# Order of the split products and a finer issue of transposes in a two-layer decoder trunk

## The chip, the cores and the metric

One core of one Trainium2 chip runs the whole program in a single launch. The metric is the device time of one execution in microseconds; the median of three runs of the kernel before is 2433.37 us (2432.49 to 2433.54).

## The reference

Two decoder layers over 256 tokens of width 2048, in float32. Layer 0 mixes with gated linear attention beside RWKV-7, layer 1 with causal softmax attention of 16 heads and an ALiBi penalty; behind each mixer stands a SwiGLU FFN with 5632 hidden columns. Cut to what matters here:

```python
h = x
for layer in range(2):
    hn = rmsnorm(h, norm_mix[layer])
    h = h + (gla_rwkv_mixer(hn, ...) if layer == 0 else moba_attention(hn, attn_qkv_w[0], attn_out_w[0]))
    h = h + swiglu(rmsnorm(h, norm_ffn[layer]), ffn_gate_w[layer], ffn_up_w[layer], ffn_down_w[layer])
return rmsnorm(h, norm_final)

def swiglu(h, w_gate, w_up, w_down):
    return (silu(h @ w_gate) * (h @ w_up)) @ w_down
```

## The kernel before, in words

**Split products.** Each weight block arrives in float32 (`raw`, L135 to L141) and is split in two: ScalarE copies it to the rounded type, `hi` (L150), and VectorE subtracts to get `lo` (L151). The activations lie split too, transposed (128 features on the partitions, 256 tokens in columns), as `xh` and `xl`. A product is the sum of three matmuls: `xh` with `hi`, `xh` with `lo`, `xl` with `hi`. In mode "x" (L170 to L172) the activation is the stationary operand (128 x 128) and the weights move (512 columns), for two token halves `t` in two PSUM tiles; in mode "w" (L177 to L180: the mixer's first projections, queries and keys) the weights are stationary and 256 tokens move.

**Jobs and units.** `run_jobs` works through a list of jobs, one for each 512 output columns of a matrix. A job has units of two 128-row weight blocks: 24 matmuls in mode "w" and 12 in mode "x". A gate or up job has 8 units, a down job of an FFN group 12 (group one: hidden tiles 0 to 5, 24 blocks) or 10 (group two: tiles 6 to 10, 20 blocks). The split of a unit is issued AHEAD = 2 units before its products; `raw` has NRAW = 4 buffers, `hi` and `lo` three each. So the split of unit n+2 reuses the buffer that unit n-1 has read. The loads go out on the SP queue.

**Side work.** Everything else (evacuating PSUM, activations, norms, transposes, attention) is written as generators. Before each unit `tick()` takes one hop of every hot generator, and hops of the others while a budget of 1.80 lasts; a `yield` says what a hop is charged. All engines run in program order, so what a hop issues stands on VectorE and ScalarE ahead of the split issued behind it. `force` ticks on until a condition holds: at a job's first unit until the job two back has been evacuated, and in a down job (`ready`) until the hidden tile whose rows the unit reads has been split.

**The FFN.** For a hidden tile j comes a gate job, whose evacuation is a Silu on ScalarE (L1009), and an up job, whose evacuation multiplies (L1014), turns the tile into `hT` with VectorE's 32 x 32 block transposes (`quads`, L257, four instructions a call, eight calls a tile) and splits `hT` into `hth` (L1027) and `htl` (L1028). This generator runs in the units of the next job. Two calls of `quads` make one hop.

**The residual and the norms.** `t_add` adds a down job's output to `h` (L954), in the last group sums the squares, and makes the next block of `xh`, `xl`. For the second mixer's norm (`gmix1`, end of layer 0) blocks 0 to 2 are turned by `quads`, block 3 by TensorE (`xt_bank`: four transposes in a PSUM bank, L242); for the FFN norms all four blocks are turned by TensorE.

Of the kernel before, what the change touches and what calls it, by code (L numbers as in the profile page):

```python
# [10 lines left out]
F32 = mybir.dt.float32  # L11
# [7 lines left out]
P = 128  # L19
S = 256  # L20
# [26 lines left out]
def tile_trunk(  # L47
# [4 lines left out]
    V, A, T, G = nc.vector, nc.scalar, nc.tensor, nc.gpsimd  # L52
# [34 lines left out]
        return dict(w=w_ap, segs=segs or [(0, c0, 512)], ncol=ncol, rows=rows, x=x, done=done, mode=mode, start=start,  # L87
                    ready=ready)

    # Side work runs as generators: each yields what its hop is charged against a step's BUDGET.  # L90
    tasks = []
    carry = [0.0]
    flags = set()
# [31 lines left out]
    def run_jobs(jobs, prologue):  # L125
        BOTH = slice(0, 2)
        units = [(jb, i) for jb in jobs for i in range(0, len(jb["rows"]), 2)]
        raws, splits = {}, {}

        def fetch(n):  # L130
            if n >= len(units):
                return
            jb, i = units[n]
            raw = wpool.tile([P, 2, 512], F32, tag="raw", name="raw", bufs=NRAW)
            r0 = jb["rows"][i][1] * P  # L135
            for dst, c0, w in jb["segs"]:
                nc.sync.dma_start(
                    raw[:, :, dst : dst + w],
                    jb["w"][r0 : r0 + 2 * P, c0 : c0 + w].rearrange("(k p) n -> p k n", p=P),
                )  # L140
            raws[n] = raw  # L141

        def split(n, ks):
            if n >= len(units):
                return
            ncol = units[n][0]["ncol"]
            if n not in splits:
                splits[n] = tuple(wpool.tile([P, 2, 512], F32R, tag=g, name=g, bufs=3) for g in ("hi", "lo"))
            (hi, lo), raw = splits[n], raws[n]
            A.activation(hi[:, ks, :ncol], raw[:, ks, :ncol], AF.Copy)  # L150
            V.tensor_sub(lo[:, ks, :ncol], raw[:, ks, :ncol], hi[:, ks, :ncol].bitcast(F32))  # L151

        def finish(jb, k):
            yield from jb["done"](jb["pt"])
            flags.add(("evac", k))

        def products(n, k, ts=(0, 1)):
            jb, i = units[n]
            hi, lo = splits[n]
            xh, xl = jb["x"]()  # L160
            nm = jb["ncol"] // P
            if i + k == 0 and 0 in ts:
                jb["pt"] = [mm_tile() for _ in range(2)]
            pt = jb["pt"]
            xi = jb["rows"][i + k][0]
            first, last = i + k == 0, i + k == len(jb["rows"]) - 1
            if jb["mode"] == "x":
                for t in ts:
                    sl = slice(t * P, t * P + P)
                    T.matmul(pt[t], xh[:, xi, sl], hi[:, k, :], start=first, stop=False)  # L170
                    T.matmul(pt[t], xh[:, xi, sl], lo[:, k, :], start=False, stop=False)  # L171
                    T.matmul(pt[t], xl[:, xi, sl], hi[:, k, :], start=False, stop=last)  # L172
            else:
                for m in range(nm):
                    o = pt[m // 2][:, (m % 2) * 256 : (m % 2) * 256 + 256]
                    ms = slice(m * P, m * P + P)
                    T.matmul(o, hi[:, k, ms], xh[:, xi, :], start=first and m % 2 == 0, stop=False,  # L177
                             skip_group_check=True)
                    T.matmul(o, hi[:, k, ms], xl[:, xi, :], start=False, stop=False, skip_group_check=True)  # L179
                    T.matmul(o, lo[:, k, ms], xh[:, xi, :], start=False, stop=last, skip_group_check=True)  # L180

        for n in range(NRAW):
            fetch(n)
        prologue()
        for n in range(AHEAD):
            split(n, BOTH)
            fetch(n + NRAW)
            if n == 0:
                spawn(t_x0(), hot=True)
                tick()  # L190
        for half in range(2):
            spawn(t_chain_when(half))
            spawn(t_rwkv_e(half), fast=lambda half=half: (("kp", half) in flags and ("dec", half) in flags
                                                          and ("pre", half) not in flags)
                  or (("neu", half) in flags and ("inv", half) not in flags))
            spawn(t_rwkv_r(half))
            spawn(t_rwkv_d(half))
        spawn(t_gate())
        spawn(t_gla())
        for n, (jb, i) in enumerate(units):  # L200
            if i == 0 and jb["start"]:
                jb["start"]()
            tick()
            if i == 0:
                k = jobs.index(jb)
                if k >= 2:
                    force(lambda: ("evac", k - 2) in flags)
            busy = any(t[2] and t[2]() for t in tasks)
            if jb["ready"]:
                force(lambda: jb["ready"](jb["rows"][i + 1][0]))  # L210
            split(n + AHEAD, slice(0, 1) if busy else BOTH)
            if not busy:
                fetch(n + AHEAD + NRAW)
            if n == len(units) - 3:
                while tasks:
                    tick()
                for t in range(2):
                    for m in range(n, n + 3):
                        for k in range(2):
                            products(m, k, (t,))  # L220
                    jb["done"](t, jb["pt"][t])
                break
            products(n, 0)
            if busy:
                mid()
                split(n + AHEAD, slice(1, 2))
                fetch(n + AHEAD + NRAW)
            products(n, 1)
            if i + 2 >= len(jb["rows"]):
                spawn(finish(jb, jobs.index(jb)), hot=True)  # L230
        while tasks:
            tick()
# [33 lines left out]
        V.tensor_scalar(dst, dst, 1.0 / D, RMS_EPS, op0=ALU.mult, op1=ALU.add)  # L266
        half_pow(dst, dst)

    # ------------------------------------------------------------ layer 0 mixer: state
    right = ExitStack()  # L270
    st = {"right": right}
    opool = right.enter_context(tc.tile_pool(name="opool", bufs=1, side="right"))
# [103 lines left out]
    def quarter(pt, p):  # L376
        return pt[p // 2][:, (p % 2) * 256 : (p % 2) * 256 + 256]

    # ------------------------------------------------------------ layer 0 mixer: tasks
    def t_lora(pt):  # L380
        wa = wt([P, S], "t1")
        g1 = wt([P, S], "t2")
# [540 lines left out]
            yield 1.8  # L923
        flags.add(("og", j))

    # ------------------------------------------------------------ residual stream
    def open_h():
        left.close()
        hpool = ctx.enter_context(tc.tile_pool(name="hpool", bufs=1, reuse_waits="tile"))
# [19 lines left out]
    def t_add(j, gname=None, last=False, final=False):  # L949
        def go(pt):  # L950
            h = st["h"]
            for t in range(2):
                hs = h[:, t, j * 512 : j * 512 + 512]
                V.tensor_add(hs, pt[t], hs)  # L954
            if gname is not None or final:
                sumsq(h, j, st["junk"])
            yield 1.3
            if final:
                cols = slice(j * 512, j * 512 + 512)
                for t in range(2):  # L960
                    V.tensor_mul(st["ob"][:, t, cols], h[:, t, cols], st["nf"][:, cols])
                yield 1.2
            if last:
                rstd_of(rst)
            if gname == "gmix1" and not last:
                hT = st["fp"].tile([P, 4, S], F32, tag="hT", name="hT", bufs=2)
                for t in range(2):
                    for i in range(4):
                        quads(hT[:, :, t * P + 32 * i : t * P + 32 * i + 32],
                              h[32 * i : 32 * i + 32, t, j * 512 : j * 512 + 512].rearrange("p (f c) -> p f c", f=4))  # L970
                        if i % 2:
                            yield 1.6
                for b in range(2):
                    xt_evac(st["xh"], st["xl"], hT[:, 2 * b : 2 * b + 2, :].rearrange("p a t -> p (a t)"),
                            4 * j + 2 * b, gname)
                    yield 1.0
            elif gname is not None:
                for b in range(2):
                    xt_bank(st["xh"], st["xl"], h, 4 * j + 2 * b, gname)
                    yield 1.0  # L980
            if last and gname == "gmix1":
                flags.add("rst1")
        return go

    def final_rows(t, ps):
        h, ob, rt = st["h"], st["ob"], rst[:, t : t + 1]
# [15 lines left out]
    def t_gate_up(layer, kind, j, g0):  # L1002
        def go(pt):
# [15 lines left out]
            for t in range(2):  # L1019
                for i in range(4):  # L1020
                    quads(hT[:, :, t * P + 32 * i : t * P + 32 * i + 32],
                          sgt[32 * i : 32 * i + 32, t, :].rearrange("p (f h) -> p f h", f=4))
                    if i % 2:
                        yield 1.6
            for b in range(2):
                f, hb = (j - g0) * 4 + 2 * b, hT[:, 2 * b : 2 * b + 2, :]
                A.activation(hth[:, f : f + 2, :], hb, AF.Copy)  # L1027
# [40 lines left out]
                                 t_add(j, gnext if g0 else None, last=bool(g0) and j == 3, final=final)))  # L1068
        return jobs

    # ------------------------------------------------------------ layer 1 attention
    def open_attn():
        st["fs"].close()
        rs = ExitStack()
# [87 lines left out]
        flags.add(("head", hd))  # L1162
        yield 0.8

    # ------------------------------------------------------------ program
    with tc.manual_schedule():
        jobs = [gemm(mix_in, 0, ALLK, xT, t_lora, mode="w", segs=[(0, 6160, 256), (256, 6384, 64), (320, 3072, 64)])]
        for half in range(2):
# [120 lines left out]
```

## Time and profile before

| what | value |
|---|---|
| median of three runs | 2433.37 us |
| profiled execution, first to last instruction | 2431.0 us |
| TensorE busy, matmuls | 2383.2 us, 98% |
| VectorE busy | 1601.4 us, 66% |
| ScalarE busy | 1071.2 us, 44% |
| bytes read from HBM | 421.34 MB, 174 GB/s with those written |

The span is that of one profiled execution; the runs' times were taken by themselves. The profile counts an engine as busy from an instruction's start to its end; the ends of matmuls are modelled and lie behind the start of the next, so an idle time of TensorE reads shorter than the delay of the start. A number in brackets behind a timeline row is the engine's idle time before it and what ended it. x8 behind a row means eight like instructions in a run.

### The profile page before, as it was taken

The numbers are of one execution on the slowest core, as the hardware profiler recorded it, in microseconds if no ns is written. First come the engines' busy times: TensorE is split into PE (matmuls) and PEld (weight loads), VectorE is DVE, ScalarE is ACT, GpSimd is POOL, SyncE is SP. The second block draws the span as 40 slices with busy tenths as digits, with TensorE's granted clock in tenths as the row PEclk, the third lists the DMA queues.
The fourth block names the chain that finished last, engine by engine and source line by source line (L and its number), as shares of the span: only waits on it lengthen the run. The fifth ranks groups of instructions, "written<-read, shape, count | busy, mean of one in ns | idle before, by whom it ended". The sixth has DMA issues, their size and how long they took to land.

```text
span 2431.0 us, 33126 instructions
## 1 busy us (share of the span) xinstructions
PE 2383.2 (98%) x12786; PEld 2017.5 (83%) x12786; DVE 1601.4 (66%) x2505; ACT 1071.2 (44%) x1380; POOL 158.4 (7%) x183
## 2 busy tenths in 40 slices
PE   8999999999999999999999999999999999999998
PEld 8999978788787888887879999978887878887876
DVE  4765864666667644677785677886667664477664
ACT  5553454454444433444444444445444433444443
POOL 2270440100000000000000000000000000000000
PEclk9999999999999999999999999999999999999999
DMA  6542543555665655665556565555665655656654
GB/s 195 151 140 84 149 145 91 169 173 182 197 189 177 199 186 187 190 189 185 180 176 191 166 182 174 167 180 182 191 190 175 198 189 184 191 185 191 193 182 156
DMA packets 224094, 425.61 MB, mean 175 GB/s; under 512 B 17600, under 2 KB 19936, under 8 KB 223808
## 3 DMA queue, kind: packets, MB, share of 16 engines
q1 hardware_dynamic: 222976, 419.66, 55.2%
q0 software_dynamic: 960, 3.83, 0.5%
q8 instruction: 100, 1.64, 0.3%
q14 instruction: 58, 0.48, 0.1%
HBM read 421.34 MB, written 2.10 MB: 174 GB/s over the span
## 4 chain that ended last, share of the span: by engine, by line
PE 74%; DVE 20%; issue 3%; ACT 2%; DMA 0%; SPq 0%; ACTq 0%; POOLq 0%; POOL 0%; DVEq 0%
PE mmt L171 19%; PE mmt L172 19%; PE mmt L170 18%; DVE hT L257 9%; DVE lo L151 8%; PE mmt L177 4%; PE mmt L180 4%; PE mmt L179 4%; DVE pT L257 2%; ACT hi L150 2%; PE auxt L600 1%; DMA raw<-in_mix_in 0%; PE auxt L639 0%; PE auxt L632 0%; PE auxt L242 0%
## 5 line engine op out<-in xcount | busy, mean ns | idle before, releaser
L151 DVE TENSOR_TENSOR lo<-raw,hi 128x1024 fp32r<-128x1024 f32 (+2 forms) x818 | 973.6, 1193 | 738.4 <-ACT hi L150 732.1
L150 ACT ACTIVATE hi<-raw 128x1024 fp32r<-128x1024 f32 (+2 forms) x818 | 837.6, 1029 | 924.3 <-PE mmt L172 801.9
L171 PE MATMUL mmt<-lo,xh 128*128 128x512 f32 x1664 | 651.2, 391 | 16.5 <-DVE lo L151 16.5
L170 PE MATMUL mmt<-hi,xh 128*128 128x512 f32 x1664 | 652.3, 392 | 0.0
L172 PE MATMUL mmt<-hi,xl 128*128 128x512 f32 x1664 | 648.8, 390 | 0.0
L171 PEld LDWEIGHTS mmt<-lo,xh 128*128 128x128 f32 x1664 | 312.8, 188 | 91.1 <-DVE lo L151 28.1
L170 PEld LDWEIGHTS mmt<-hi,xh 128*128 128x128 f32 x1664 | 312.7, 188 | 65.6
L172 PEld LDWEIGHTS mmt<-hi,xl 128*128 128x128 f32 x1664 | 312.8, 188 | 64.1
L177 PE MATMUL mmt<-xh,hi 128*128 128x256 f32 x1072 | 312.9, 292 | 2.4 <-DVE xl L252 2.2
L180 PE MATMUL mmt<-xh,lo 128*128 128x256 f32 x1072 | 304.4, 284 | 4.1 <-DVE lo L151 4.1
L179 PE MATMUL mmt<-xl,hi 128*128 128x256 f32 x1072 | 303.6, 283 | 0.0
L171 PE MATMUL mmt<-lo,hth 128*128 128x512 f32 x704 | 280.3, 398 | 5.2 <-DVE lo L151 5.2
L170 PE MATMUL mmt<-hi,hth 128*128 128x512 f32 x704 | 279.1, 396 | 0.0
L172 PE MATMUL mmt<-hi,htl 128*128 128x512 f32 x704 | 279.0, 396 | 0.0
L257 DVE STREAM_TRANSPOSE hT<-sgt 32x128 f32<-32x128 f32 x704 | 212.8, 302 | 9.8
L180 PEld LDWEIGHTS mmt<-xh,lo 128*128 128x128 f32 x1072 | 205.7, 192 | 5.6 <-DVE lo L151 5.6
L177 PEld LDWEIGHTS mmt<-xh,hi 128*128 128x128 f32 x1072 | 205.8, 192 | 5.0 <-ACT hi L150 2.0
L179 PEld LDWEIGHTS mmt<-xl,hi 128*128 128x128 f32 x1072 | 205.9, 192 | 0.8
L171 PEld LDWEIGHTS mmt<-lo,hth 128*128 128x128 f32 x704 | 132.6, 188 | 41.9 <-DVE lo L151 10.2
L170 PEld LDWEIGHTS mmt<-hi,hth 128*128 128x128 f32 x704 | 132.6, 188 | 32.3
L172 PEld LDWEIGHTS mmt<-hi,htl 128*128 128x128 f32 x704 | 132.6, 188 | 31.8
L257 DVE STREAM_TRANSPOSE pT<-lg 32x96 f32<-32x96 f32 x256 | 69.0, 269 | 3.8
(291 smaller groups left out, 1667.8 us busy)
## 6 DMA issues: line engine op xcount, KB each, us to landing
raw<-in_wg SPq DMA_DIRECT2D x176, 512.0 KB, 3.5
raw<-in_wu SPq DMA_DIRECT2D x176, 512.0 KB, 3.6
raw<-in_wd SPq DMA_DIRECT2D x176, 512.0 KB, 3.6
raw<-in_mix_in SPq DMA_DIRECT2D x96, 512.0 KB, 3.6
raw<-in_qkv SPq DMA_DIRECT2D x96, 512.0 KB, 4.0
raw<-in_mix_out SPq DMA_DIRECT2D x32, 512.0 KB, 3.6
raw<-in_attn_out SPq DMA_DIRECT2D x32, 512.0 KB, 3.7
arz<-in_x SPq DMA_DIRECT2D x8, 256.0 KB, 5.8
```

The lines of the kernel that those rows point to most:

```text
L150: A.activation(hi[:, ks, :ncol], raw[:, ks, :ncol], AF.Copy)
L151: V.tensor_sub(lo[:, ks, :ncol], raw[:, ks, :ncol], hi[:, ks, :ncol].bitcast(F32))
L170: T.matmul(pt[t], xh[:, xi, sl], hi[:, k, :], start=first, stop=False)
L171: T.matmul(pt[t], xh[:, xi, sl], lo[:, k, :], start=False, stop=False)
L172: T.matmul(pt[t], xl[:, xi, sl], hi[:, k, :], start=False, stop=last)
L177: T.matmul(o, hi[:, k, ms], xh[:, xi, :], start=first and m % 2 == 0, stop=False, skip_group_check=True)
L179: T.matmul(o, hi[:, k, ms], xl[:, xi, :], start=False, stop=False, skip_group_check=True)
L180: T.matmul(o, lo[:, k, ms], xh[:, xi, :], start=False, stop=last, skip_group_check=True)
L257: V.transpose(dst[32 * q : 32 * q + 32], src[:, :, 32 * q : 32 * q + 32])
L600: T.matmul(psA[p // 2][:, (p % 2) * 256 : (p % 2) * 256 + 256], bk[:, p, c, :], arz[:, p, c, :, :], start=True, stop=True)
```

## The change

In mode "x" each weight block's four products with `hi` come first (both token halves), then the two with `lo`. The hop of the FFN tile's transposes has one call of `quads` and is charged 1.3. Of the blocks of the second mixer norm, block 0 is turned by `quads` in a hot generator of its own that does nothing in every other tick; blocks 1 and 2 go through `xt_bank`, as block 3 did. Some comment lines are taken out.

```diff
@@ products
                 for t in ts:
                     sl = slice(t * P, t * P + P)
                     T.matmul(pt[t], xh[:, xi, sl], hi[:, k, :], start=first, stop=False)
-                    T.matmul(pt[t], xh[:, xi, sl], lo[:, k, :], start=False, stop=False)
-                    T.matmul(pt[t], xl[:, xi, sl], hi[:, k, :], start=False, stop=last)
+                    T.matmul(pt[t], xl[:, xi, sl], hi[:, k, :], start=False, stop=False)
+                for t in ts:
+                    sl = slice(t * P, t * P + P)
+                    T.matmul(pt[t], xh[:, xi, sl], lo[:, k, :], start=False, stop=last)
@@ t_add
-            if gname == "gmix1" and not last:
-                hT = st["fp"].tile([P, 4, S], F32, tag="hT", name="hT", bufs=2)
-                for t in range(2):
-                    for i in range(4):
-                        quads(hT[:, :, t * P + 32 * i : t * P + 32 * i + 32],
-                              h[32 * i : 32 * i + 32, t, j * 512 : j * 512 + 512].rearrange("p (f c) -> p f c", f=4))
-                        if i % 2:
-                            yield 1.6
-                for b in range(2):
-                    xt_evac(st["xh"], st["xl"], hT[:, 2 * b : 2 * b + 2, :].rearrange("p a t -> p (a t)"),
-                            4 * j + 2 * b, gname)
-                    yield 1.0
+            if gname == "gmix1" and j == 0:
+                spawn(t_quads(gname), hot=True)
             elif gname is not None:
                 for b in range(2):
                     xt_bank(st["xh"], st["xl"], h, 4 * j + 2 * b, gname)
@@ new
+    def t_quads(gname):
+        h = st["h"]
+        hT = st["fp"].tile([P, 4, S], F32, tag="hT", name="hT", bufs=2)
+        for t in range(2):
+            for i in range(4):
+                yield 0
+                quads(hT[:, :, t * P + 32 * i : t * P + 32 * i + 32],
+                      h[32 * i : 32 * i + 32, t, 0:512].rearrange("p (f c) -> p f c", f=4))
+                yield 1.3
+        for b in range(2):
+            xt_evac(st["xh"], st["xl"], hT[:, 2 * b : 2 * b + 2, :].rearrange("p a t -> p (a t)"), 2 * b, gname)
+            yield 1.0
@@ t_gate_up
                 for i in range(4):
                     quads(hT[:, :, t * P + 32 * i : t * P + 32 * i + 32],
                           sgt[32 * i : 32 * i + 32, t, :].rearrange("p (f h) -> p f h", f=4))
-                    if i % 2:
-                        yield 1.6
+                    yield 1.3
```

## Rows read from the trace of the kernel before

**Rows 1.** The page's engine table: busy us, share of the span, instructions.
```profile
PE 2383.2 (98%) x12786; PEld 2017.5 (83%) x12786; DVE 1601.4 (66%) x2505; ACT 1071.2 (44%) x1380; POOL 158.4 (7%) x183
```

**Rows 2.** The page's costliest groups: count, busy, mean ns, idle before, releaser.
```profile
L171 PE MATMUL mmt<-lo,xh 128*128 128x512 f32 x1664 | 651.2, 391 | 16.5 <-DVE lo L151 16.5
```

**Rows 3.** TensorE's waits, whole span: us in total, times, longest us.
```profile
PE mmt L171 <- DVE lo L151: 23.3, 30, 2.2
```

**Rows 4.** TensorE's waits, four stretches in order: 552:816, 816:952, 952:1174, 1174:1293.
```profile
PE mmt L171 <- DVE lo L151: 4.0, 5, 0.8
...
PE mmt L171 <- DVE lo L151: 0.3, 1, 0.3
...
PE mmt L171 <- DVE lo L151: 3.2, 4, 0.8
...
PE mmt L171 <- DVE lo L151: 4.3, 7, 0.7
```

**Rows 5.** TensorE's timeline, gate and up tiles: start us, us, instruction, count [idle].
```profile
699.96 0.50 PE L171 MATMUL mmt<-lo,xh 128*128 128x512 f32 x1 [0.80 <-DVE lo L151]
...
742.34 0.39 PE L171 MATMUL mmt<-lo,xh 128*128 128x512 f32 x1
742.57 0.39 PE L172 MATMUL mmt<-hi,xl 128*128 128x512 f32 x1
...
743.47 0.39 PE L170 MATMUL mmt<-hi,xh 128*128 128x512 f32 x1
744.66 0.50 PE L171 MATMUL mmt<-lo,xh 128*128 128x512 f32 x1 [0.80 <-DVE lo L151]
```

**Rows 6.** VectorE's timeline, 733 to 749 us, the same tile.
```profile
739.57 1.23 DVE L151 TENSOR_TENSOR lo<-raw,hi 128x1024 fp32r<-128x1024 f32 x1
740.82 2.52 DVE L257 STREAM_TRANSPOSE hT<-sgt 32x128 f32<-32x128 f32 x8
743.38 1.23 DVE L151 TENSOR_TENSOR lo<-raw,hi 128x1024 fp32r<-128x1024 f32 x1
744.52 1.29 DVE L1028 TENSOR_TENSOR htl<-hT,hth 128x512 fp32r<-128x512 f32 x2
```

**Rows 7.** ScalarE's timeline, 738 to 758 us, the same tile.
```profile
743.38 1.15 ACT L1027 ACTIVATE hth<-hT 128x512 fp32r<-128x512 f32 x2 [4.13 <-DVE hT L257]
...
747.52 1.06 ACT L150 ACTIVATE hi<-raw 128x1024 fp32r<-128x1024 f32 x1 [1.09 <-PE mmt L172]
749.57 1.37 ACT L1009 ACTIVATE sgt<-mmt,rst 128x512 f32<-128x512 f32 x2 [0.98 <-PE mmt L172]
```

**Rows 8.** TensorE's timeline, two successive down jobs that end layer 0.
```profile
1217.98 0.50 PE L171 MATMUL mmt<-lo,hth 128*128 128x512 f32 x1 [0.60 <-DVE lo L151]
...
1248.02 0.50 PE L171 MATMUL mmt<-lo,hth 128*128 128x512 f32 x1 [0.60 <-DVE lo L151]
```

**Rows 9.** TensorE's timeline around one bank of transposes, 1661 to 1663 us.
```profile
1661.11 0.39 PE L172 MATMUL mmt<-hi,aol 128*128 128x512 f32 x1
...
1661.81 0.40 PE L172 MATMUL mmt<-hi,aol 128*128 128x512 f32 x1
1662.05 0.60 PE L242 MATMUL auxt<-cs__68,h 128*128 128x128 f32 x4
...
1662.71 0.40 PE L171 MATMUL mmt<-lo,aoh 128*128 128x512 f32 x1
```

**Rows 10.** Windows: us, busy of PE, PEld, DVE, ACT, POOL, PEclk, DMA, GB/s.
```profile
323.40:326.80 3.40, 3.40 (x10) 2.62 (x9) 2.14 (x2) 2.78 (x4) 3.12 (x4) 0.50 0.62 172
...
500.00:556.00 56.00, 56.00 (x260) 45.50 (x259) 36.21 (x48) 30.74 (x53) 0.70 (x1) 1.00 0.53 173
```

**Rows 11.** TensorE's timeline, 320 to 327 us, a value job of layer 0.
```profile
323.00 0.50 PE L171 MATMUL mmt<-lo,xh 128*128 128x512 f32 x1 [2.25 <-DVE lo L151]
...
324.10 0.63 PE L171 MATMUL mmt<-lo,xh 128*128 128x512 f32 x1
324.53 0.63 PE L172 MATMUL mmt<-hi,xl 128*128 128x512 f32 x1
```

**Rows 12.** TensorE's timeline, 1618 to 1622 us, attention's output projection.
```profile
1620.44 0.50 PE L171 MATMUL mmt<-lo,aoh 128*128 128x512 f32 x1 [1.58 <-DVE lo L151]
```

## The prediction

> **What bounds the kernel now.** I read the page's engine table first: TensorE is busy for 2383.2 of 2431.0 us [rows 1]. That number does not say how much can be won, because matmul records overlap: one 512-column matmul is recorded with 391 ns [rows 2], but in a quiet stretch the fifth after one at 742.34 starts at 743.47 [rows 5], 0.227 us each. So I go by start-to-start times. The kernel ends when TensorE has issued its matmuls, and only what lengthens that pitch costs time.
>
> Next, TensorE's waits. The one large entry is L171 (the low half of the split weights) waiting for VectorE's `lo`: 23.3 us in 30 waits [rows 3]. Asked by stretch, they sit in the first FFN and its end: five in gate/up tiles 0 to 5, one in the first down job, four in the second group's gate/up, seven in its down jobs [rows 4]. Layer 1 repeats the first three stretches with the same counts and times (its last down jobs, without the mixer norm, have only one wait).
>
> The timelines show why. In every gate/up tile VectorE runs eight 32x32-block transposes (2.50 us), then the next unit's `lo` (1.23 us): start to start 3.8 us, four units in a row [rows 6], while TensorE takes twelve matmuls, 12 x 0.227 = 2.72 us. VectorE falls behind by about 1.1 us a unit; with two units split ahead, the fourth is too late. L171 then starts 1.19 us after L170 instead of 0.227 [rows 5].
>
> **The change part by part.** The sum is against the profiled execution: its span is 2431.0 us; the median of the runs is 2433.37 us. I carry the 2.4 us between them unchanged.
>
> *Transposes four at a time (FFN tiles).* VectorE's unit becomes 4 x 0.313 + 1.23 = 2.5 us, under 2.72: it no longer falls behind. Price of one stall: two consecutive stalled matmuls stand at 699.96 and 744.66, 44.70 us apart [rows 5]; a tile has 16 units, 192 x 0.2267 = 43.52 us. So 1.18 us a tile, including the slow matmuls just behind the stall. 5 + 4 tiles per layer, 18 in all: -21.2 us. The wait in the first down job of each of four groups is shorter (0.3 us idle [rows 4] against 0.80; I price it 0.64, an estimate that takes off the 0.5 less of idling, its unit being 12 x 0.234 = 2.81 us): -2.6 us.
>
> What takes the place? Eight hops plus the first (the multiply), the split into high and low, and a last one that sets the flag make 11 ticks; a gate job has 8 units. So at unit 0 of the next up job the eighth hop is issued, and the demand that the job two back be evacuated forces the split into the same unit. There ScalarE has the Silu pair 1.37 us, the `hth` pair 1.15 and a `hi` of 1.06 [rows 7], then comes `lo` with 1.23: 4.8 us from the unit's start. That `lo` is first used two units and, in the new order, four matmuls later: 2 x 2.72 + 0.91 = 6.35 us. It is covered by 1.5 us; I cost it at nothing, and if the cover went, at up to the old 1.18 us a tile.
>
> In a group's first down job there is a real new wait. Group one has 24 rows; its last tile's rows are read at unit 10 and the split comes at unit 9: nothing. Group two has 20 rows; its last tile is read at unit 8, whose own tick issues the eighth hop, and the forced tick puts the split behind it. Worked out: `hi` of the unit ahead starts when its buffer is freed; 1.06 of `hi`, 1.23 of `lo` and 1.25 of four transposes are 3.54 us against a unit of 2.81; the transposes end 0.3 (buffer freed two matmuls earlier by the new order) to 0.7 us into unit 8. Then one `hth` (half of the 1.15 pair, 0.62 with its start) and one `htl` (half of the pair's 1.29 [rows 6], 0.69 with its start): TensorE's second matmul waits 1.5 to 2.0 us, with the slow restart about 1.9. Two layers: +3.8 us. Bounds: 0, if the queue has run ahead, and 2 x 2.8 us, a whole unit each; I take the middle, from the nearest rows. Queued behind on TensorE is everything; on ScalarE the next `hi`, due two units on.
>
> *Second mixer norm.* Three of the four down jobs that end layer 0 now have the same eight-at-a-time transposes of `h`, and two waits each, the first 0.60 us idle. Stalled matmuls of successive jobs stand at 1217.98 and 1248.02 [rows 8], 30.04 us; a job is 10 units x 12 x 0.234 = 28.1. So 1.93 us a job, -5.8 us. Block 0 stays with VectorE, one hop of four in every second tick: 16 ticks and two splits, from unit 2 of the second job to unit 9 of the third. In the third job VectorE also adds block 1, two 512-column operations that I price like the two of `htl`, 1.29, and makes its `xl`: units 0 to 2 carry some 8.3 us against 3 x 2.81; covered. Blocks 1 and 2 become 16 TensorE transposes in four banks. One such bank already stands in attention's last jobs: from L172 at 1661.81 to L171 at 1662.71 is 0.90 us where two pitches would be 0.47 [rows 9]: 0.43 a bank, +1.7 us. They read `h` added one unit earlier, so no wait: `h` is ready 1.3 us into a unit of 2.81.
>
> The granted clock is 1.00 over 500 to 556 us, where eight such banks run among matmuls [rows 10]; so no clock price. The Trainium skill ("TensorE: Matmul & The Clock Gate", Part 4: PE-mode transpose) says that the transpose mode does not count as busy TensorE in the same way, which would speak against moving transposes there; the trace does not show such a loss for banks of four between matmuls. By that rule it is a rival below.
>
> *Low half last.* All matmuls stay, and the weight loads. From L171 to L172 it is 0.23 and over the four starts behind that, which take in the step to the other PSUM tile and the same `xh` loaded twice, 0.90 [rows 5]: every kind of neighbour in the new order stands in the old one at one pitch, so I cost the order at nothing. The bounds are a loss of the two stages' difference in pitch (rival 3) and no gain. It lets `lo` be three matmuls later, 0.68 us. In the FFN the transposes have already removed the stall. Elsewhere two remain: 2.25 us idle at 323.00 [rows 11] and 1.58 at 1620.44 [rows 12], VectorE being busy with scans and attention's transposes; and some 0.4 us ahead of the latter. -1.8 us. After the first, eight matmuls go at 0.43 [rows 11] with the granted clock at 0.50, the half level, 1.2 GHz [rows 10], because TensorE had stood still before: 1.6 us more. Whether a wait shortened to 1.6 us still loses it no row shows: between 0 and -1.8; I take -0.9. The SP queue fetches when `lo` frees a `raw` buffer: with VectorE even, sooner, not later.
>
> Sum: -21.2 - 2.6 + 3.8 - 5.8 + 1.7 - 1.8 - 0.9 = -26.8. Span 2404.2, time 2406.6 us.
>
> **The rivals.**
> 1. *The stall returns at the up job's first unit* (Silu, `hth`, `hi`, `lo` in one row on ScalarE). For it: two hops in one unit, and today `hth` waits 4.13 us on ScalarE ahead of a `hi` [rows 7]. Against: 1.5 us of cover. Half of the 18 stalls back: 2406.6 + 10.6 = 2417.
> 2. *The clock falls at the moved transposes* (the page's rule as a mechanism here): each of four banks costs a stretch like that behind 323.00, 1.7 us: 2413. Against: the 1.00 around eight present banks.
> 3. *Slower: the new order loses the fast pitch in the gate, up and value jobs.* The same instructions of the same shape go at 0.227 there and 0.234 in attention's output and the down jobs (1661.11 to 1661.81, three pitches) [rows 5, 9], and the trace does not say why; 3 x 1664 matmuls [rows 2] at +7.6 ns are +37.9 us: 2444.5. It decides from 5.4 ns a matmul, where the gain is eaten. Against: within a stage the pitch is the same for all three pairs of neighbours.
> 4. *It does not do what it says*: the waits are put down to `lo` but another resource, unchanged, would be late next (ScalarE's `hi`, a landing): 2433. Against: each stall stands just behind four runs of eight transposes, and ends when that `lo` does.
> 5. *More*: the new down-job wait is hidden and the clock loss goes whole: 2402.
>
> **How the numbers follow.** Forecast 75% (its own range 2403 to 2412), rival 1 10%, rival 2 4%, rival 3 4%, rival 4 3%, rival 5 4%. The range 2402 to 2418 holds the forecast, 1 and 2 and leaves out some 15%. About 0.2% (4.9 us) is what a measurement of this kernel can tell from no change. Faster: forecast, 1, 2 and 5, less the tail of 1: 0.91. Same: rival 4 and that tail: 0.05. Slower: 0.04.
>
> **What would show it.** Right: in the gate/up tiles L257 stands in runs of four, stalled matmuls are gone and a tile repeats every 43.5 us; a wait of TensorE for `htl` of 1.5 to 2 us at unit 8 of both second groups' first down job; down jobs at the end of layer 0 of 28.1 and twice 29 us; 88 transposes at L242's line instead of 72; the wait near 323 us shorter by 0.7. Wrong: waits for `lo` with a period of a tile, or a pitch of 0.234 in gate and up jobs, or a 0.50 clock near 1240 us.

## The result, and the profile after

The changed kernel takes 2407.44 us (median) against 2432.93 us for the kernel before, timed beside it: a ratio of 0.9896, 95% interval 0.9882 to 0.9910. Predicted were 2406.6 us. The profiled execution spans 2406.3 us against 2431.0. One of the six executions of the last kernel below took 13404.72 us, for which no run shows a reason; the median given there is that of all six, the ratio leaves it out.

The largest wait before was 23.3 us in 30 waits of TensorE for `lo` [rows 3]. This is the same view of the changed kernel, in us, times, longest; L174 is now the low half, L170 and L171 the two products with `hi`:

```profile
PE auxt L548 <- DVE DX L544: 4.9, 2, 3.1
PE mmt L182 <- DVE lo L151: 4.2, 6, 0.8
PE mmt L174 <- DVE lo L151: 3.2, 2, 1.8
...
PE mmt L170 <- ACT hth L1031: 2.2, 2, 1.1
...
PE mmt L171 <- DVE htl L1032: 0.5, 2, 0.2
```

The 30 waits for `lo` in mode "x" are two, and four short ones for `hth` and `htl` are new. VectorE's timeline of a hidden tile, against the runs of eight in [rows 6]:

```profile
738.32 1.25 DVE L259 STREAM_TRANSPOSE hT<-sgt 32x128 f32<-32x128 f32 x4
739.78 1.23 DVE L151 TENSOR_TENSOR lo<-raw,hi 128x1024 fp32r<-128x1024 f32 x1 [0.22 <-ACT hi L150]
741.04 1.25 DVE L259 STREAM_TRANSPOSE hT<-sgt 32x128 f32<-32x128 f32 x4
742.50 1.23 DVE L151 TENSOR_TENSOR lo<-raw,hi 128x1024 fp32r<-128x1024 f32 x1 [0.21 <-ACT hi L150]
743.76 1.26 DVE L259 STREAM_TRANSPOSE hT<-sgt 32x128 f32<-32x128 f32 x4
746.17 1.29 DVE L1032 TENSOR_TENSOR htl<-hT,hth 128x512 fp32r<-128x512 f32 x2 [1.16 <-ACT hth L1031]
747.64 1.23 DVE L151 TENSOR_TENSOR lo<-raw,hi 128x1024 fp32r<-128x1024 f32 x1 [0.18 <-ACT hi L150]
```

Each `lo` is now preceded by an idle time that ScalarE's `hi` ends, and that `hi` waits for TensorE, which frees its buffer. ScalarE's timeline of the same tile:

```profile
738.69 1.06 ACT L150 ACTIVATE hi<-raw 128x1024 fp32r<-128x1024 f32 x1 [1.66 <-PE mmt L171]
```

So VectorE is ahead and goes at TensorE's pace: `lo` to `lo` is 2.72 us, TensorE's unit. The last three rows of VectorE are the up job's first unit, rival 1's place. There the split waits 1.16 us behind the Silu pair and `lo` comes late, but nobody waits for it: between 552 and 946 us TensorE has no wait at all.

The larger of the two that are left, TensorE's timeline in the value job (before, [rows 11]):

```profile
320.89 0.39 PE L171 MATMUL mmt<-hi,xl 128*128 128x512 f32 x1
323.12 0.96 PE L174 MATMUL mmt<-lo,xh 128*128 128x512 f32 x2 [1.83 <-DVE lo L151]
323.87 0.63 PE L170 MATMUL mmt<-hi,xh 128*128 128x512 f32 x1
324.30 0.63 PE L171 MATMUL mmt<-hi,xl 128*128 128x512 f32 x1
```

Three matmuls that used to stand behind the wait now stand ahead of it. Behind it the pitch is again 0.43 us, with the granted clock at the half level (0.51, the first window further below). The idle time itself fell only from 2.25 to 1.83 us and not by the 0.7 that the prediction gave as a sign: before, an earlier `lo` in the same job had come 0.13 us late (309.23 to 309.58), which with its slow restart cost some 0.26 us, and that delay is gone too, so that TensorE comes to the wait sooner.

The new wait, TensorE's timeline in the second group's first down job at unit 8:

```profile
1184.26 0.63 PE L174 MATMUL mmt<-lo,hth 128*128 128x512 f32 x2
1185.97 0.49 PE L170 MATMUL mmt<-hi,hth 128*128 128x512 f32 x1 [1.09 <-ACT hth L1031]
1186.70 0.50 PE L171 MATMUL mmt<-hi,htl 128*128 128x512 f32 x1 [0.23 <-DVE htl L1032]
```

L170 waits for `hth`, the next matmul for `htl`; with the slow restart (the start behind a matmul that waited is 0.34 us away and not 0.23) this job loses 1.83 us. The moved transposes, and the clock over all four down jobs that end layer 0 (columns as in [rows 10]):

```profile
1222.64 0.63 PE L174 MATMUL mmt<-lo,hth 128*128 128x512 f32 x2
1223.11 0.60 PE L244 MATMUL auxt<-cs__68,h 128*128 128x128 f32 x4
1223.46 0.48 PE L170 MATMUL mmt<-hi,hth 128*128 128x512 f32 x1
1223.78 0.40 PE L171 MATMUL mmt<-hi,htl 128*128 128x512 f32 x1
```
```profile
323.40:326.80 3.40, 3.40 (x9) 2.63 (x9) 2.03 (x2) 3.12 (x5) 3.09 (x5) 0.51 0.66 166
1161.00:1290.00 129.00, 127.68 (x602) 104.64 (x601) 88.37 (x141) 58.45 (x78) 1.53 (x3) 1.00 0.55 180
```

From L244 at 1223.11 to L171 at 1223.78 is 0.67 us, where one pitch would be 0.23: 0.44 for the bank, against 0.43 in attention [rows 9]. The clock stays at 1.00.

Every job has the same matmuls in both kernels, so the starts of each job's first matmul, in both traces, give the change term by term:

| term | predicted, us | measured, us | how |
|---|---|---|---|
| stall in each of 18 hidden tiles | -21.2 | -20.8 | 1.13 to 1.18 each; a tile now 43.52 |
| old wait in four first down jobs | -2.6 | -2.2 | 34.29 to 33.74; 28.66 to 28.11 without the new wait |
| new wait in two of them | +3.8 | +3.7 | 29.94 and 29.95 against 28.11 |
| norm: stalls of three down jobs | -5.8 | -5.8 | 30.03 to 28.11 |
| norm: four banks on TensorE | +1.7 | +1.7 | 28.98 and 28.96 against 28.11 |
| low half last, elsewhere | -1.8 | -1.3 | -0.68 and -0.16 in the value jobs, -0.49 in attention |
| half clock behind the first of these | -0.9 | -0.2 | the rest of -0.89 in that job |
| sum | -26.8 | -24.9 | span -24.7 |

Jobs not named here differ by 0.03 us at most. One caution for spans: the start of the program differs between executions of any of these kernels (the first job takes 20.9 to 22.5 us), so the terms are read from the jobs, not from spans. The same holds for the two value jobs, by more than their terms in this table: over the eight kernels here with the new order, whose programs are the same up to there, the first took 24.1 to 25.5 us and the second 29.2 to 31.0. So -0.16 in the second is not shown to come from the order.

### The profile page after: what moved, and what is told of

The parts are those of the page before. It is cut to its first block, busy times and chain, and to the rows that moved or that the text cites. A ratio compares the mean times of both kernels' runs of the same rounds, so it can differ in the third digit from the quotient of the medians.

```text
span 2406.3 us, 33103 instructions
## 1 busy us (share of the span) xinstructions
PE 2376.2 (99%) x12802; PEld 2022.6 (84%) x12802; DVE 1588.7 (66%) x2441; ACT 1068.0 (44%) x1380; POOL 159.9 (7%) x183
## 4 chain that ended last, share of the span: by engine, by line
PE 92%; DVE 5%; issue 1%; ACT 1%; DMA 0%; SPq 0%; ACTq 0%; POOLq 0%; POOL 0%; DVEq 0%
PE mmt L170 25%; PE mmt L171 24%; PE mmt L174 24%; PE mmt L179 4%; PE mmt L182 4%; PE mmt L181 4%; DVE lo L151 2%; DVE pT L259 2%; PE auxt L602 1%; ACT hi L150 1%; DMA raw<-in_mix_in 0%; PE auxt L244 0%; PE auxt L634 0%; PE auxt L641 0%; PE auxt L666 0%
## 5 line engine op out<-in xcount | busy, mean ns | idle before, releaser
L170 PE MATMUL mmt<-hi,xh 128*128 128x512 f32 x1664 | 652.5, 392 | 0.0
L171 PE MATMUL mmt<-hi,xl 128*128 128x512 f32 x1664 | 648.6, 390 | 0.0
L174 PE MATMUL mmt<-lo,xh 128*128 128x512 f32 x1664 | 513.4, 390 | 1.8 <-DVE lo L151 1.8
L174 PEld LDWEIGHTS mmt<-lo,xh 128*128 128x128 f32 x1664 | 312.6, 188 | 67.7 <-DVE lo L151 2.3
L170 PEld LDWEIGHTS mmt<-hi,xh 128*128 128x128 f32 x1664 | 313.0, 188 | 64.7
L171 PEld LDWEIGHTS mmt<-hi,xl 128*128 128x128 f32 x1664 | 313.2, 188 | 64.4
L170 PE MATMUL mmt<-hi,hth 128*128 128x512 f32 x704 | 279.6, 397 | 2.2 <-ACT hth L1031 2.2
L171 PE MATMUL mmt<-hi,htl 128*128 128x512 f32 x704 | 279.3, 397 | 0.5 <-DVE htl L1032 0.5
L174 PE MATMUL mmt<-lo,hth 128*128 128x512 f32 x704 | 222.9, 396 | 0.0
L170 PEld LDWEIGHTS mmt<-hi,hth 128*128 128x128 f32 x704 | 132.6, 188 | 35.0 <-ACT hth L1031 3.0
L171 PEld LDWEIGHTS mmt<-hi,htl 128*128 128x128 f32 x704 | 132.6, 188 | 33.1 <-DVE htl L1032 1.1
L174 PEld LDWEIGHTS mmt<-lo,hth 128*128 128x128 f32 x704 | 132.6, 188 | 32.3
```

## The experiments

Each was timed beside the kernel before (2431.2 to 2431.4 us in those sets). They ask what each part is worth beside the others, what the new wait hangs on, and, at the end, what rival 3 had left unexplained.

**The old order back.**

```diff
                     T.matmul(pt[t], xh[:, xi, sl], hi[:, k, :], start=first, stop=False)
-                    T.matmul(pt[t], xl[:, xi, sl], hi[:, k, :], start=False, stop=False)
-                for t in ts:
-                    sl = slice(t * P, t * P + P)
-                    T.matmul(pt[t], xh[:, xi, sl], lo[:, k, :], start=False, stop=last)
+                    T.matmul(pt[t], xh[:, xi, sl], lo[:, k, :], start=False, stop=False)
+                    T.matmul(pt[t], xl[:, xi, sl], hi[:, k, :], start=False, stop=last)
```

> The changed kernel with the old order of the products (high, low, high per token half). Theory: VectorE's work per unit (four transposes and lo, 2.5 us) fits under TensorE's 2.72 us in any order, so the gate/up tiles stay at 43.5 us; what comes back is the 0.89 + 0.16 us in the value job, the 0.49 in attention's output and some 0.25 us in each second group's first down job: +2 us, about 2409.5. Rival (the low half's later need is what took the stalls away): the tile stalls return, 18 x 1.15 us, about 2428.

Measured 2409.58 us (0.9910, 0.9896 to 0.9925). No tile changes (43.52 us); what comes back is 0.89 and 0.14 us in the value jobs, 0.49 in attention's output, 0.26 and 0.24 in the two first down jobs: 2.0 us. The rival falls: with the hops of four, the order is worth 2 us of 25, and only half of that is sure, since the 1.0 us in the value jobs is no more than these jobs differ by between executions of one program.

**The hops of eight back**, in the FFN tiles alone.

```diff
-                    yield 1.3
+                    if i % 2:
+                        yield 1.6
```

> The changed kernel with the FFN tile's transposes given out eight at a time again. Theory A: VectorE is late by a fixed time of 0.96 us at the fourth unit and the new order asks for lo 0.68 us later, so 0.28 us of stall and 0.15 of slow restart stay in each of 18 tiles, +8 us; the new wait in the second groups' first down job goes, -3.6: about 2412. Theory B: the high buffer that is freed two matmuls earlier lets VectorE make up another 0.45 us, the stalls are gone altogether and only the new wait goes: about 2403.8, and the hops of four cost time. Theory C (the order is worth nothing in the FFN): +20.8 - 2.6: 2425.6.

Measured 2411.58 us (0.9916, 0.9902 to 0.9931). TensorE's timeline of a tile:

```profile
608.09 0.39 PE L171 MATMUL mmt<-hi,xl 128*128 128x512 f32 x1
608.72 0.73 PE L174 MATMUL mmt<-lo,xh 128*128 128x512 f32 x2 [0.23 <-DVE lo L151]
```

The start is delayed by 0.63 - 0.23 = 0.40 us where it was 0.96, and every tile is 0.46 to 0.57 us longer than 43.52; the new wait is gone (28.11 us both). That is theory A, though it gave 0.28 for the delay. So the two edits overlap: the new order alone would have taken more than half of each tile's stall, the hops of four take all of it with either order.

**The norm back on VectorE**, blocks 0 to 2 in hops of eight.

```diff
-            if gname == "gmix1" and j == 0:
-                spawn(t_quads(gname), hot=True)
+            if gname == "gmix1" and not last:
+                hT = ...
+                        quads(...)
+                        if i % 2:
+                            yield 1.6
+                for b in range(2):
+                    xt_evac(...)
+                    yield 1.0
```

> The changed kernel with blocks 0 to 2 of the second mixer norm turned by VectorE, eight transposes a hop, as before. Theory A (only the later need of lo counts): stalls of 0.77 and 0.91 us shrink by 0.68 each, about 0.5 us a job with restarts stays in three jobs, against 0.87 us in two jobs for TensorE's transposes: 2407.2, no difference. Theory B (the earlier freed buffer counts too): no stalls, -1.7: 2405.7. Theory C (order worth nothing here): +4.0: 2411.4.

Measured 2410.82 us (0.9913, 0.9898 to 0.9928); the three down jobs take 29.68 to 29.69 us, 1.57 over 28.11, where theory A gave 0.5 and the old order had 1.92. None of the three theories holds: the time is nearest to theory C (2411.4), but by the jobs the order is worth 0.35 us in each and not nothing. VectorE's and TensorE's timelines of the first:

```profile
1191.83 1.29 DVE L956 TENSOR_TENSOR h<-mmt,h 128x512 f32<-128x512 f32 x2 [0.68 <-PE mmt L174]
...
1202.37 1.23 DVE L151 TENSOR_TENSOR lo<-raw,hi 128x1024 fp32r<-128x1024 f32 x1
1203.51 2.50 DVE L259 STREAM_TRANSPOSE hT<-h 32x128 f32<-32x128 f32 x8
1206.04 1.23 DVE L151 TENSOR_TENSOR lo<-raw,hi 128x1024 fp32r<-128x1024 f32 x1
1207.30 2.52 DVE L259 STREAM_TRANSPOSE hT<-h 32x128 f32<-32x128 f32 x8
1209.86 1.23 DVE L151 TENSOR_TENSOR lo<-raw,hi 128x1024 fp32r<-128x1024 f32 x1
```
```profile
1207.32 0.73 PE L174 MATMUL mmt<-lo,hth 128*128 128x512 f32 x2 [0.31 <-DVE lo L151]
1211.14 0.73 PE L174 MATMUL mmt<-lo,hth 128*128 128x512 f32 x2 [0.74 <-DVE lo L151]
```

I had taken the later need off each of the two waits. It counts once: after the first wait TensorE goes on at VectorE's pace, and the second is the difference of the two, `lo` to `lo` 3.82 us (1206.04 to 1209.86) against a unit of 2.81. And of the 0.70 us half is given back: the first token half's sum is finished two matmuls later, so the adds of `h` start where the next job does (1191.83 against its first matmul at 1191.87), while in the kernel before they started 0.38 ahead of it. VectorE's and TensorE's timelines there:

```profile
1202.50 1.28 DVE L954 TENSOR_TENSOR h<-mmt,h 128x512 f32<-128x512 f32 x2
1202.88 0.39 PE L170 MATMUL mmt<-hi,hth 128*128 128x512 f32 x1
```

This account adds up (0.70 less 0.34 is 0.36, and 0.35 came), but no run tests it by itself.

**The last tile sooner.** The last hidden tile of the second group has two hops of eight, then four of four.

```diff
-                    yield 1.3
+                    if j < NF - 1 or t or i % 2:
+                        yield 1.3
```

> The changed kernel, where the last hidden tile of the second group has its first four calls of transposes in two hops of eight and the rest in hops of four. Its split then comes at unit 7 of the first down job, ahead of the need at unit 8; two units of eight transposes put VectorE behind by 2 x 0.95 us, less than the 3 us that it can be late. Theory: the wait for hth and htl goes, 1.83 us in each of two layers: 2403.8. Rival (that wait is that of the job's start, not of the hops): 2407.4.

Measured 2402.67 us (0.9883, 0.9866 to 0.9899). VectorE's timeline in the job shows the two runs of eight go by without harm:

```profile
1160.93 2.51 DVE L259 STREAM_TRANSPOSE hT<-sgt 32x128 f32<-32x128 f32 x8
1163.48 1.22 DVE L151 TENSOR_TENSOR lo<-raw,hi 128x1024 fp32r<-128x1024 f32 x1
1164.73 2.53 DVE L259 STREAM_TRANSPOSE hT<-sgt 32x128 f32<-32x128 f32 x8
...
1178.47 1.28 DVE L1033 TENSOR_TENSOR htl<-hT,hth 128x512 fp32r<-128x512 f32 x2
```

Both first down jobs fall to 28.11 us, with no wait of TensorE there: 3.7 us. The new wait was the count of hops, as the prediction said. The time is 1.1 us below the theory, and that is not this edit's: the kernel before took some 1.5 us less in this set than beside the changed kernel, and in the profiled execution the two value jobs, which the edit does not touch, took 1.45 us less.

**All of the norm's three blocks on VectorE, in fours**, on top of that.

```diff
-            if gname == "gmix1" and j == 0:
-                spawn(t_quads(gname), hot=True)
+            if gname == "gmix1" and not last:
+                hT = ...
+                        quads(...)
+                        yield 1.3
+                for b in range(2):
+                    xt_evac(...)
+                    yield 1.0
```

> As e4_last_tile_sooner, and blocks 0 to 2 of the second mixer norm are all turned by VectorE, four transposes a hop in every tick (no TensorE transposes for blocks 1 and 2, block 0 no longer in every other tick). Theory (it is eight transposes beside lo in one unit that make VectorE late; four and lo, 2.5 us, fit under 2.81): no stall in the three down jobs, 28.1 us each, and the 0.87 us of the two jobs with TensorE transposes go: 1.7 us under e4, about 2402 against its 2403.7 (after less 3.7). Rival (the xh and xl pieces on top make VectorE late anyway): waits for lo of about 1 us in each of the three jobs, 1.3 us over e4.

Measured 2402.52 us (0.9884, 0.9871 to 0.9898), no gain that a time could show. By jobs: the third down job gains 0.86 us (28.12), the fourth with the start of the next loses 0.80 (29.76), the next job gains 0.35. TensorE's timeline there:

```profile
1273.41 0.33 PE L244 MATMUL auxt<-cs__68,h 128*128 128x128 f32 x1 [0.58 <-DVE h L956]
1274.00 0.55 PE L244 MATMUL auxt<-cs__68,h 128*128 128x128 f32 x3 [0.27 <-DVE h L956]
```

This is neither theory: there is no wait for `lo`. But block 2's generator now needs 12 ticks, one more than the ten of the next job's units and the one at the first unit behind layer 0. There `force` takes the twelfth, and so block 3's transposes stand right behind the adds of `h` that they read. The demand on the job two back, harmless in rival 1's place, costs here because what it pulls forward is TensorE's own work; the last experiment takes that tick away.

**The hidden tiles at the other end of the memory.** Rival 3 rested on a pitch of 0.227 in some jobs and 0.234 in others that the trace did not explain. `xh` and `xl` lie in pools at the left end, as the weights do; `hth`, `htl`, attention's output and the mixers' outputs at the right.

```diff
+            st["fl"] = fs.enter_context(tc.tile_pool(name=f"ffnl{layer}", bufs=1, reuse_waits="tile"))
...
-            st["ht"] = (st["fp"].tile([P, 24, S], F32R, tag="hth", name="hth"),
-                        st["fp"].tile([P, 24, S], F32R, tag="htl", name="htl"))
+            st["ht"] = (st["fl"].tile([P, 24, S], F32R, tag="hth", name="hth"),
+                        st["fl"].tile([P, 24, S], F32R, tag="htl", name="htl"))
```

> The changed kernel, with the tiles hth and htl in a pool at the left end of the memory, where xh and xl lie, and not at the right; nothing else. It asks why the same matmul goes at 0.227 us in gate and up jobs and 0.234 in down jobs. Theory L (the place of the stationary operand): 2112 matmuls at 7.6 ns less, 16 us: about 2391, down jobs of 32.6 and 27.2 us. Theory N (something else about these jobs): 2407.4, down jobs of 33.74 and 28.11 us.

Measured 2390.48 us (0.9835, 0.9822 to 0.9849). TensorE's timeline of a down job, of this kernel and then of the changed one:

```profile
860.67 0.39 PE L170 MATMUL mmt<-hi,hth 128*128 128x512 f32 x1
...
862.03 0.39 PE L170 MATMUL mmt<-hi,hth 128*128 128x512 f32 x1
```
```profile
860.26 0.40 PE L170 MATMUL mmt<-hi,hth 128*128 128x512 f32 x1
...
861.67 0.40 PE L170 MATMUL mmt<-hi,hth 128*128 128x512 f32 x1
```

Six matmuls take 1.36 us at the left and 1.41 at the right. Down jobs go from 33.74 to 32.64 and from 28.11 to 27.20 us. Theory L, to the digit.

**All of it together.** e6 with the hidden tiles at the left.

> e6_norm_in_fours with the hidden tiles at the left end as in e7_hidden_left: all that is expected to help. Under theory L 16 us below e6, about 2386; under theory N the same as e6, about 2402.

Measured 2386.32 us (0.9817, 0.9804 to 0.9830), 16.2 us under e6 in the same set: theory L again.

**Attention's output at the left as well, and one hop less in block 2.**

```diff
-        st["ao"] = (ap_.tile([P, KC, S], F32R, name="aoh"), ap_.tile([P, KC, S], F32R, name="aol"))
+        al = rs.enter_context(tc.tile_pool(name="attnl", bufs=1, reuse_waits="tile"))
+        st["ao"] = (al.tile([P, KC, S], F32R, name="aoh"), al.tile([P, KC, S], F32R, name="aol"))
...
-                    yield 1.0
+                    if j < 2 or b:
+                        yield 1.0
```

> e8_all with two more edits: attention's split output (aoh, aol) also at the left end, and the two splits of block 2 of the second mixer norm in one hop. Theory for the first: 384 matmuls at 7.6 ns less, 2.9 us, all in the eight jobs of attention's output projection. Theory for the second: in e6 the force at the first unit behind layer 0 asked for one tick too many and pulled the transposes of block 3 up against the adds of h (TensorE waiting 0.8 us for h at that line); with one hop less nothing is forced, the wait goes and the last down job falls by 1.2 to 1.6 us with the next job's start. Together about 2382. Rivals: the attention jobs stay as they are; the wait for h stays.

Measured 2382.86 us (0.9799, 0.9787 to 0.9812), the fastest version: 2% under the kernel before, some 24 us under the changed one. The wait for `h` is gone and the last down job with the job behind it takes 51.54 us against 52.92: -1.4. Attention's jobs fall by 0.13 to 0.41 us each, but the third rises by 0.20 (17.09 to 17.29): TensorE comes sooner to a `lo` that VectorE makes at its own pace, and waits longer (the late start there stands 2.01 us behind the one before it, against 1.78). So it is -1.6 in all, not -2.9. The theory had left out what breaks a job up: the fifth job, in which nothing stands between its 36 matmuls, falls by its full 0.27, but the three behind it, with two banks of transposes each, by 0.13 to 0.14. Behind a bank, ten starts take 2.31 us with the operand at the left too, against 2.27 in the undisturbed job.

## Why the prediction was right

*What bounds the kernel.* Right: start-to-start times of TensorE, not its busy share. That share went from 98 to 99% while the time fell by 1%, and the busy time fell by 7.0 us alone (2383.2 to 2376.2); the gain stood in the delayed starts of the matmuls with `lo`. The terms missed their sum by 1.9 us and the time came within 0.8 of the forecast; that second closeness is luck, within what executions of one kernel differ by.

*The tile stalls.* Right in cause and size. The price read from two stalled matmuls a tile apart took in the slow restart and held to 2%. My text said that the hops of four remove the FFN's stall whatever the order, and the first experiment shows it; the second shows that the order alone would have taken more than half of it, which the text did not price. The shorter wait in four first down jobs, priced at 0.64 us by an estimate, measured 0.55.

*The cover at the up job's first unit.* Right: the split waits there, and no wait of TensorE follows in any tile.

*The new wait.* Right in place, in cause and in size, 1.83 us against 1.9; but the larger part stands at the unit's first matmul, for `hth` (1.09 us idle), where the text had all of it at the second, for `htl` (0.23). The term came from counting ticks against units, not from any row; the fourth experiment takes it away by changing that count.

*The norm.* Right in both terms, -5.8 and +1.7, the second from the price of a bank in other jobs. The granted clock is 1.00 from 1161 to 1290 us, with the four moved banks in it. The Trainium skill ("TensorE: Matmul & The Clock Gate", Part 4: PE-mode transpose) says that the transpose mode does not count as busy TensorE in the same way; no loss by that shows here.

*Low half last.* This is the mis-sized term: -1.5 with the clock, against -2.7. In the value job TensorE gains just the three pitches (0.68). But the half clock came behind the wait all the same, and only 0.2 us less of it was paid. Whether it comes is not settled by the length of the wait. TensorE's timeline of the same place in the second experiment, whose program is the changed kernel's up to there, and a window behind it (columns as in [rows 10]):

```profile
322.60 0.73 PE L174 MATMUL mmt<-lo,xh 128*128 128x512 f32 x2 [1.85 <-DVE lo L151]
323.17 0.39 PE L170 MATMUL mmt<-hi,xh 128*128 128x512 f32 x1
323.40 0.40 PE L171 MATMUL mmt<-hi,xl 128*128 128x512 f32 x1
```
```profile
322.90:326.30 3.40, 3.40 (x16) 2.79 (x15) 2.03 (x2) 3.40 (x5) 3.09 (x5) 1.00 0.69 169
```

After 1.85 us of idling the clock stays at 1.00 there, and the job takes 24.1 us, 1.35 less than in the changed kernel; the profiled execution of "All of it together" has the same there. So my half of the clock's price stood for something that differs between executions of one program. Both executions with the old order fell to the half level at that place and took 56.6 us for the two value jobs together, the eight with the new one 54.1 to 55.6; how much of that difference the order makes, so few executions do not show. In attention I had counted three pitches for the wait and 0.4 us for a small delay ahead of it. But both belong to one chain of `lo`s that VectorE makes without a pause, 4.65 us from one to the next, so the 0.70 us counts once; and that chain stands 0.21 us later against the job's first matmul than before (1600.03 and 1600.60, before 1614.51 and 1615.29), so 0.49 came, not 1.1.

*Rival 3* fell: the pitch in the gate and up jobs is 0.2267 us as before. What it rested on is now traced to the place of the stationary operand, and no further.

## What to carry to other kernels

Where a helper engine works in units beside the main one, add up what it does in one unit and compare that with the unit's length; when it is over, hand its side work out in smaller hops, and then count the hops against the units before the first reader, and against every point that forces them. In these runs a later need for an operand was worth its distance once in a chain of late units, not once for each, and what finishes later in exchange is to be taken off. Compare the start-to-start times of the same instruction between stages: a difference of 3% in pitch was worth as much as two thirds of this change.

## What was not expected of the hardware

In an undisturbed stretch the matmul of 128 x 128 by 512 columns in the rounded type starts every 0.2267 us with its stationary operand in the left pools and every 0.234 us with it in the right pools, with the same instructions in the same order: 2112 matmuls, 16 us. Behind a wait or a bank of transposes some ten matmuls go at about 0.231 us at the left as well. The runs show that the place decides; why, and whether the end, the address or the distance from the moving operand counts, they leave open, as they do whether the tiles that shift with it in the right pools have a part.
